# Rebuilding residual rows on ScalarE from kept norm statistics, and issuing their loads from SyncE

## The chip, the core and the metric

The kernel runs on one core of one Trainium2 chip. The metric is the device time of one execution in microseconds (us). Three timed runs of the kernel before gave 821.04, 821.12 and 822.54 us, so the median is 821.12 us. Each engine of the core has its own queue, worked in order: TensorE (PE in the profile, its weight loads PEld), VectorE (DVE), ScalarE (ACT), GpSimd (POOL) and SyncE (SP), which here only issues DMAs. An engine other than PE can issue DMAs too; the profile shows such issues as ACTq or SPq.

## The reference

One decoder layer with three sub-layers, on 512 rows of width 1024, each of the form `h <- LayerNorm(ALPHA * h + f(h))`, behind a first norm:

```python
def layer_norm(x, g, b):
    xf = x.astype(jnp.float32)
    mu = jnp.mean(xf, axis=-1, keepdims=True)
    var = jnp.mean(jnp.square(xf - mu), axis=-1, keepdims=True)
    return ((xf - mu) * lax.rsqrt(var + LN_EPS) * g + b).astype(x.dtype)

    h = layer_norm(x, ln_in_g, ln_in_b)
    f = hybrid_mixer(h, ...)      # gated linear attention, indexed sparse attention, stick-breaking
    h = layer_norm(ALPHA * h + f, ln_mix_g, ln_mix_b)
    f = mem_attn(h, mem, w_mem_q, w_mem_kv, w_mem_o)          # 4 heads, 256 memory tokens
    h = layer_norm(ALPHA * h + f, ln_mem_g, ln_mem_b)
    f = sq_relu_mlp(h, w_up, b_up, w_down, b_down)            # hidden width 4096
    h = layer_norm(ALPHA * h + f, ln_ffn_g, ln_ffn_b)
```

What the change touches is the first `h`. It is used twice: transposed, as the input of all mixer projections, and much later in rows, times ALPHA, as the residual of the first sub-layer.

## The kernel before, in words

The 512 tokens are four tiles of 128 rows (NT = 4), the 1024 features eight tiles (NK = 8). An fp32 operand is split into a high part (`h_...`, fp32r) and a low remainder (`l_...`), and each product is three matmuls: high by high, high by low, low by high. Making the low part of a weight is a subtraction of a 128x1024 tile on DVE or POOL; the high part is a cast on ACT, POOL or DVE.

The program does not emit its instructions as it is written. `Program.record` and `either` (L172 on) collect every operation with its dependencies, a cost and a place in the written order; `issue` (L240 to L357) then plans greedily with those costs and emits each engine's queue in the planned order, all from L356. Some operations may run on two or three engines (`either`), and the planner picks the one that would end first. So a changed operation can move others, on every engine.

The stages in time order are: the first norm with its transposes (`x`, `ps_lt`, `h0T`) and the first projections (`ps_ik_iw`, `ps_iq`), to about 25 us; the mixer's attention groups to about 310 us, with the projections of the memory tokens woven into the end of them (`ps_vm`, `ps_km`, weights `kvv`, `kvk`); output projection and second norm (`ps_wo`); cross-attention over the memory (`ps_q`, `ps_ms`, `ps_mpt`, `ps_wmo`); third norm; the MLP (`ps_up`, `ps_dn`) to 812 us; the last norm.

The places that the change touches:

- `ln_hat` (L521): row statistics of a 128x1024 tile (two BN_STATS of 512 columns, one aggregation, an added epsilon on DVE, a power on POOL), then `center`, one DVE instruction over 128x1024 that subtracts the mean and multiplies by the scale `rs`. At the start it runs on `x_pg[t]` (L563), in place; `ln_transposed` (L529) transposes the result on PE, applies gain and shift (`h`, on ACT or DVE) and splits it into `h0T`.
- The residual (L1137 to L1144): since the rows of `x` were given up, each tile of `x` is loaded again into a page `res`, `ln_hat(p, "again")` repeats statistics and centering, and `gain_shift` (L1130) multiplies by a row of gains (`gbc_in`) and adds a row of shifts (`bbc_in`), each 128x1024.
- `gb_rows` (L548) loads such rows of gains and shifts for each of the four norms by a broadcast DMA issued by ScalarE; POOL scales them by ALPHA. `bd` (L1206) is one more such row.

Pages of 128x1024 come from one pool of 31; raw weight tiles (`r_...`) from a pool of four. A DMA into such a buffer waits at the head of its issuing engine's queue until the earlier user of the buffer is done.

Of the kernel before, what the change touches and what calls it, by code (L numbers as in the profile page):

```python
# [9 lines left out]
F32 = mybir.dt.float32  # L10
F32R = mybir.dt.float32r
U32 = mybir.dt.uint32
AF = mybir.ActivationFunctionType
OP = mybir.AluOpType
# [3 lines left out]
T, D = 512, 1024  # L18
# [346 lines left out]
def trunk_kernel(ctx: ExitStack, tc: tile.TileContext, x, mem, ln_in_g, ln_in_b, w_in, gate_w2,  # L365
# [3 lines left out]
    x, mem, out = x[0], mem[0], out[0]  # L369
# [5 lines left out]
    def pool(name, tag, bufs, space=None):  # L375
        kw = {"space": space} if space else {}
        got = ctx.enter_context(tc.tile_pool(name=name, bufs=bufs or 1, **kw))
        return VPool(got, tag, bufs, space is PSUM)

    cst = pool("cst", None, 0)  # L380
# [8 lines left out]
    nc = Program(real)  # L389
    slack = [0.0]  # L390

    def page(shape, dtype, name):
        return pages.tile([128] + shape, dtype, name)

    def temp(name, n=512, dtype=F32):
        return half.tile([128, n], dtype, name)
# [7 lines left out]
    def pool_tt(o, a, b, op):  # L404
        nc.gpsimd.tensor_tensor(o, a, b, op=op)
# [89 lines left out]
    x_pg = []  # L495
    for t in range(NT):
        p = page([D], F32, f"x{t}")
# [10 lines left out]
    def mean_scale(st, name):  # L508

        mv = tiny(2, "mv_" + name)  # L510
        nc.vector.bn_aggr(mv, st)
        ve = tiny(1, "ve_" + name)
        nc.vector.tensor_scalar(ve, mv[:, 1:2], EPS, None, op0=OP.add)
        rs = tiny(1, "rs_" + name)
        nc.gpsimd.tensor_tensor(rs, ve, mhalf[:, 0:1], op=OP.pow)
        return mv, rs

    def center(y, mv, rs):
        nc.vector.tensor_scalar(y, y, mv[:, 0:1], rs, op0=OP.subtract, op1=OP.mult)

    def ln_hat(y, name):  # L521

        st = small.tile([128, 2, 6], F32, "st_" + name)
        for c in range(2):
            nc.vector.bn_stats(st[:, c, :], y[:, 512 * c:512 * c + 512])
        mv, rs = mean_scale(st, name)
        center(y, mv, rs)

    def ln_transposed(hat, g, b, hT, t0, n):  # L529

        w = 128 * n
        for k0 in range(0, NK, 512 // w):
            kk = 512 // w
            ps = bank("ps_lt", (kk, w))
            for k in range(kk):
                for t in range(n):
                    nc.tensor.transpose(ps[:, k, 128 * t:128 * t + 128],
                                        hat[t0 + t][:, 128 * (k0 + k):128 * (k0 + k) + 128], ident)
            for k in range(kk):
                kt = k0 + k  # L540
                cols = slice(128 * t0, 128 * t0 + w)
                h32 = temp("h32")[:, :w]
                gs, bs = g[:, kt:kt + 1], b[:, kt:kt + 1]
                nc.either(("scalar", "activation", (h32, ps[:, k, :], AF.Identity), dict(bias=bs, scale=gs)),
                          ("vector", "tensor_scalar", (h32, ps[:, k, :], gs, bs), dict(op0=OP.mult, op1=OP.add)))
                split(hT[kt][:, 0, cols], hT[kt][:, 1, cols], h32)

    def gb_rows(g, b, scale, name):  # L548
        res = []
        for nm, v in (("g", g), ("b", b)):  # L550
            p = page([D], F32, f"{nm}bc_{name}")
            nc.scalar.dma_start(p, v.to_broadcast([128, D]))
            if scale != 1.0:
                nc.gpsimd.tensor_scalar(p, p, scale, 0.0, op0=OP.mult, op1=OP.add)
            res.append(p)
        return res

    def new_hT(name):
        return [page([2, T], F32R, f"{name}{k}") for k in range(NK)]


    hT = new_hT("h0T")
    for t in range(NT):  # L563
        ln_hat(x_pg[t], "in")
        if t % 2:
            ln_transposed(x_pg, *gb_cols["in"], hT, t - 1, 2)

# [126 lines left out]
    for j in range(1, NT):  # L694
# [3 lines left out]
        for h in range(IDX_H):  # L698
# [7 lines left out]
            else:  # L706
                nc.vector.scalar_tensor_tensor(acc[:, :n], r[:, :n], iw[:, j, h:h + 1], acc[:, :n],
                                               op0=OP.mult, op1=OP.add)
# [103 lines left out]
    for b in range(NT):  # L812
# [8 lines left out]
        v = gv[b // 2][:, b % 2, :]  # L821
# [308 lines left out]
    def gain_shift(hat, gb, t, later=0.0):  # L1130
        nc.clock += later
        any_tt(hat[t], hat[t], gb[0], OP.mult)
        any_tt(hat[t], hat[t], gb[1], OP.add)
        nc.clock -= later


    gb = gb_rows(ln_in_g[None, :], ln_in_b[None, :], ALPHA, "in")  # L1137
    res = []
    for t in range(NT):
        p = page([D], F32, f"res{t}")  # L1140
        nc.scalar.dma_start(p, x[128 * t:128 * t + 128, :])
        ln_hat(p, "again")
        res.append(p)
        gain_shift(res, gb, t)  # L1144
    h1T = new_hT("h1T")
# [5 lines left out]

    gemm_tok(mix, w_out, 0, NK, "wo", after_mix)
    gb = gb_rows(ln_mix_g, ln_mix_b, ALPHA, "mix")
    for t in range(NT):
        gain_shift(res, gb, t, GAIN_LATER)
# [3 lines left out]
    for h in range(MEM_H):  # L1159
# [10 lines left out]
        for t in range(NT):  # L1170
# [8 lines left out]
            p = temp("mp")  # L1179
# [22 lines left out]

    gemm_tok(oT, w_mem_o, 0, NK, "wmo", after_mem)
    gb = gb_rows(ln_mem_g, ln_mem_b, ALPHA, "mem")
    bd = page([D], F32, "bd")
    nc.scalar.dma_start(bd, b_down.to_broadcast([128, D]))  # L1206
    pool_tt(gb[1], gb[1], bd, OP.add)
    for t in range(NT):
        gain_shift(res, gb, t, GAIN_LATER)
# [207 lines left out]
```

## Time and profile before

| | value |
|---|---|
| median of three timed runs | 821.12 us (821.04 to 822.54) |
| the profiled execution | 822.55 us |
| its span, first to last instruction | 820.8 us |
| outside the span | 1.75 us |
| mean granted TensorE clock | 0.990 of full |
| PE busy | 790.4 us, 96% |
| DVE busy | 636.3 us, 78% |
| ACT busy | 328.0 us, 40% |
| POOL busy | 144.5 us, 18% |

The profiled execution is one run, 1.43 us over the median of the timed ones. All durations below are from it. Busy times add up what each engine worked on; a share of 96% for PE leaves 30.4 us of the span in which it ran no matmul.

### The profile page before, as it was taken

The numbers are of one execution on the slowest core, as the hardware profiler recorded it, in microseconds if no ns is written. First come the engines' busy times: TensorE is split into PE (matmuls) and PEld (weight loads), VectorE is DVE, ScalarE is ACT, GpSimd is POOL, SyncE is SP. The second block draws the span as 40 slices with busy tenths as digits, with TensorE's granted clock in tenths as the row PEclk, the third lists the DMA queues.
The fourth block names the chain that finished last, engine by engine and source line by source line (L and its number), as shares of the span: only waits on it lengthen the run. The fifth ranks groups of instructions, "written<-read, shape, count | busy, mean of one in ns | idle before, by whom it ended". The sixth has DMA issues, their size and how long they took to land.

```text
span 820.8 us, 11293 instructions
## 1 busy us (share of the span) xinstructions
PE 790.4 (96%) x4177; PEld 662.5 (81%) x4177; DVE 636.3 (78%) x1118; ACT 328.0 (40%) x631; POOL 144.5 (18%) x169
## 2 busy tenths in 40 slices
PE   7999999999999999999999989999999999899995
PEld 5998768777877888899788888888888888678884
DVE  7737999997649984776953778997777776798778
ACT  5506634577535540244340233223323332585430
POOL 5320141354622210120530120000000000110001
PEclk8999999999999999999999999999999999999998
DMA  8520331603244535041322025466546555467632
GB/s 232 145 54 15 100 94 27 180 9 102 70 139 162 159 139 155 27 127 54 129 77 78 26 78 164 133 216 201 184 148 211 202 167 170 147 214 243 195 126 103
DMA packets 99927, 106.70 MB, mean 130 GB/s; under 512 B 10448, under 2 KB 79136, under 8 KB 99872
## 3 DMA queue, kind: packets, MB, share of 16 engines
q1 hardware_dynamic: 97344, 99.00, 38.5%
q10 hardware_dynamic: 2528, 6.98, 2.5%
q8 instruction: 33, 0.54, 0.3%
q14 instruction: 22, 0.18, 0.1%
HBM read 94.69 MB, written 10.49 MB: 128 GB/s over the span
## 4 chain that ended last, share of the span: by engine, by line
PE 69%; DVE 16%; issue 3%; ACT 1%; POOL 1%; DVEq 0%; ACTq 0%; POOLq 0%
PE ps_up L356 21%; PE ps_dn L356 18%; PE ps_wo L356 5%; PE ps_wmo L356 4%; PE ps_q L356 4%; DVE acc L356 2%; DVE m L356 2%; PE ps_km L356 2%; DVE res L356 2%; PE ps_z L356 2%; PE ps_vm L356 2%; PE ps_dq L356 1%; DVE s L356 1%; PE ps_mo L356 1%; PE ps_ms L356 1%
## 5 line engine op out<-in xcount | busy, mean ns | idle before, releaser
L356 PE MATMUL ps_up<-h2T,h_up 128*128 128x512 f32 (+1 forms) x576 | 163.1, 368 | 0.4 <-POOL h2T L356 0.4
L356 PEld LDWEIGHTS ps_up<-h2T,h_up 128*128 128x128 f32 x576 | 105.4, 191 | 18.2 <-POOL h2T L356 0.6
L356 PE MATMUL ps_up<-h2T,l_up 128*128 128x512 f32 (+1 forms) x288 | 105.9, 368 | 0.0
L356 ACT ACTIVATE ur<-ps_up,gb_all 128x512 f32<-128x512 f32 x32 | 22.1, 690 | 103.6 <-PE ps_up L356 103.4
L356 PEld LDWEIGHTS ps_up<-h2T,l_up 128*128 128x128 f32 x288 | 55.0, 191 | 8.6
L356 PE MATMUL ps_dn<-h_dn,a 128*128 128x512 f32 x192 | 59.2, 389 | 0.0
L356 DVE TENSOR_TENSOR l_dn<-r_dn,h_dn 128x1024 fp32r<-128x1024 f32 (+1 forms) x44 | 45.2, 1027 | 4.9 <-ACT h_dn L356 3.5
L356 PE MATMUL ps_dn<-h_dn,ends 128*128 128x512 f32 x128 | 47.0, 390 | 0.7 <-DVE ends L356 0.7
L356 POOL TENSOR_TENSOR a<-keep,a 128x1024 fp32r<-128x1024 f32 x1 | 4.9, 4924 | 229.9 <-DVE l_dn L356 229.9
L356 PE MATMUL ps_q<-h1T,h_wmq 128*128 128x256 f32 (+1 forms) x192 | 44.7, 323 | 0.3 <-POOL h1T L356 0.3
L356 PEld LDWEIGHTS ps_dn<-h_dn,a 128*128 128x128 f32 x192 | 36.0, 188 | 7.4
L356 ACT ACTIVATE h<-ps_lt,gb_all 128x256 f32<-128x256 f32 x18 | 9.1, 566 | 80.3 <-PE ps_lt L356 80.3
L356 PE MATMUL ps_wmo<-h_wmo,oT 128*128 128x512 f32 x128 | 40.8, 393 | 0.0
L356 PE MATMUL ps_wo<-h_wo,mix 128*128 128x512 f32 x128 | 40.3, 392 | 0.0
L356 DVE TENSOR_TENSOR l_up<-r_up,h_up 128x1024 fp32r<-128x1024 f32 x31 | 37.8, 1223 | 1.9 <-ACT h_up L356 0.5
L356 PE MATMUL ps_dn<-l_dn,a 128*128 128x512 f32 x96 | 37.3, 389 | 0.0
L356 PEld LDWEIGHTS ps_q<-h1T,h_wmq 128*128 128x128 f32 x192 | 32.0, 190 | 2.8 <-POOL h1T L356 0.6
L356 DVE TENSOR_SCALAR h_up<-r_up 128x1024 fp32r<-128x1024 f32 x19 | 13.1, 692 | 22.7 <-PE ps_up L356 16.4
L356 PE MATMUL ps_q<-h1T,l_wmq 128*128 128x256 f32 (+1 forms) x96 | 30.7, 320 | 0.0
L356 PEld LDWEIGHTS ps_dn<-h_dn,ends 128*128 128x128 f32 x128 | 24.0, 188 | 6.1 <-DVE ends L356 1.2
L356 PEld LDWEIGHTS ps_wo<-h_wo,mix 128*128 128x128 f32 x128 | 24.0, 188 | 4.9
L356 PEld LDWEIGHTS ps_wmo<-h_wmo,oT 128*128 128x128 f32 x128 | 24.0, 188 | 4.8
(407 smaller groups left out, 2085.2 us busy)
## 6 DMA issues: line engine op xcount, KB each, us to landing
r_dn<-in_w_down_dram SPq DMA_DIRECT2D x48, 512.0 KB, 4.3
r_up<-in_w_up_dram SPq DMA_DIRECT2D x32, 512.0 KB, 4.2
r_t<-t SPq DMA_DIRECT2D x16, 512.0 KB, 4.1
r_kvv<-in_w_mem_kv_dram SPq DMA_DIRECT2D x8, 512.0 KB, 4.3
r_kvk<-in_w_mem_kv_dram SPq DMA_DIRECT2D x8, 512.0 KB, 3.6
r_wo<-in_w_out_dram SPq DMA_DIRECT2D x8, 512.0 KB, 4.6
r_wmq<-in_w_mem_q_dram SPq DMA_DIRECT2D x8, 512.0 KB, 5.2
r_wmo<-in_w_mem_o_dram SPq DMA_DIRECT2D x8, 512.0 KB, 3.2
```

Of the source, the lines that this page charges most:

```text
L356: f(*[real(a) for a in args], **{k: real(a) for k, a in kwargs.items()})
```

## The change

Four things are edited. The first norm now keeps, for each row tile, two columns `kept` = (scale, -mean * scale), made by two DVE instructions of one column right after the centering. The residual rows are no longer normalised again from their own statistics: after the load, one ScalarE instruction computes `scale * x + (-mean * scale)` in place. The loads of the residual rows and of the rows of gains and shifts, and of `bd`, are issued by SyncE, 13 DMAs in all. Tiles get a name of their own per row tile.

```diff
@@ ln_hat
         mv, rs = mean_scale(st, name)
         center(y, mv, rs)
+        kept = cst.tile([128, 2], F32, "kept_" + name)
+        nc.vector.tensor_scalar(kept[:, 1:2], mv[:, 0:1], rs, -1.0, op0=OP.mult, op1=OP.mult)
+        nc.vector.tensor_copy(kept[:, 0:1], rs)
+        return kept
@@ gb_rows
-            nc.scalar.dma_start(p, v.to_broadcast([128, D]))
+            nc.sync.dma_start(p, v.to_broadcast([128, D]))
@@ first norm
+    norms = []
     for t in range(NT):
-        ln_hat(x_pg[t], "in")
+        norms.append(ln_hat(x_pg[t], f"in{t}"))
@@ residual
         p = page([D], F32, f"res{t}")
-        nc.scalar.dma_start(p, x[128 * t:128 * t + 128, :])
-        ln_hat(p, "again")
+        nc.sync.dma_start(p, x[128 * t:128 * t + 128, :])
+        nc.scalar.activation(p, p, AF.Identity, bias=norms[t][:, 1:2], scale=norms[t][:, 0:1])
         res.append(p)
         gain_shift(res, gb, t)
@@ before the third norm
-    nc.scalar.dma_start(bd, b_down.to_broadcast([128, D]))
+    nc.sync.dma_start(bd, b_down.to_broadcast([128, D]))
```

The planner makes a new order out of this. On DVE, at the start of the program, from the centering of row tile 0 (`x_86`) to the first low parts of the transposed input (`h0T`), it was:

```order
L356 TENSOR_SCALAR x_86<-x_86,mv_in,rs_in 128x1024
L356 TENSOR_TENSOR l_ik_iw<-r_ik_iw,h_ik_iw 128x8x72
L356 TENSOR_SCALAR x_91<-x_91,mv_in,rs_in 128x1024
L356 BN_STATS st_in<-x_103 128x6
L356 TENSOR_TENSOR l_iq<-r_iq,h_iq 128x1024
L356 TENSOR_SCALAR h0T_203<-h_190 128x256
L356 TENSOR_SCALAR h0T_205<-h_197 128x256
L356 TENSOR_TENSOR h0T_203<-h_190,h0T_203 128x256
```

In the changed kernel the same stretch of DVE, between the same two points, is:

```order
L356 TENSOR_SCALAR x_86<-x_86,mv_in_147,rs_in_159 128x1024
L356 TENSOR_SCALAR kept_in_166<-mv_in_147,rs_in_159 128x1
L356 COPY kept_in_166<-rs_in_159 128x1
L356 TENSOR_TENSOR l_ik_iw<-r_ik_iw,h_ik_iw 128x8x72
L356 TENSOR_SCALAR x_91<-x_91,mv_in_157,rs_in_169 128x1024
L356 TENSOR_SCALAR kept_in_184<-mv_in_157,rs_in_169 128x1
L356 COPY kept_in_184<-rs_in_169 128x1
L356 BN_STATS st_in_187<-x_103 128x6
L356 TENSOR_SCALAR h_196<-ps_lt,gb_in 128x256
L356 TENSOR_SCALAR h_205<-ps_lt,gb_in 128x256
L356 TENSOR_SCALAR h_213<-ps_lt,gb_in 128x256
L356 TENSOR_SCALAR h_217<-ps_lt,gb_in 128x256
```

Two `kept` instructions stand ahead of row tile 1's centering and two behind it. The low part `l_iq` has left the stretch (POOL makes it, right behind its two powers), and four `h` tiles that stood on ACT or later on DVE now stand ahead of the first low part of `h0T`, which is the next instruction.

On SP, from the last weight of the mixer (`r_dv`) to the weights of the memory's keys (`r_kvk`), minus is before and plus is now; `r_kvv` are the weights of the memory's values:

```order
 L356 DMA r_dv<-in_w_in_dram 128x8x128
-L356 DMA r_kvv<-in_w_mem_kv_dram 128x2x512 x8
+L356 DMA r_kvv<-in_w_mem_kv_dram 128x2x512 x4
+L356 DMA gbc_in<-in_ln_in_g_dram 128x1024
+L356 DMA bbc_in<-in_ln_in_b_dram 128x1024
+L356 DMA res_2606<-in_x_dram 128x1024
+L356 DMA res_2608<-in_x_dram 128x1024
+L356 DMA res_2610<-in_x_dram 128x1024
+L356 DMA res_2612<-in_x_dram 128x1024
+L356 DMA r_kvv<-in_w_mem_kv_dram 128x2x512 x4
 L356 DMA r_kvk<-in_w_mem_kv_dram 128x8x128 x8
```

Six loads now stand in the middle of the eight `r_kvv` loads. The pages of `gbc_in` and `bbc_in` come free with the transposes of the memory tokens (`ps_mt`), those of `res` with the last readers of `h0T`, the `ps_dv` matmuls.

On DVE in the residual stage, from the first statistics of a residual tile to the first added shift, it was:

```order
L356 BN_STATS st_again<-res_2608 128x6
L356 TENSOR_TENSOR vm_2707<-ps_vm,vm_2687 128x512
L356 BN_STATS st_again<-res_2608 128x6
L356 TENSOR_TENSOR vm_2723<-ps_vm,vm_2711 128x512
L356 BN_AGGR mv_again<-st_again 128x2
L356 BN_STATS st_again<-res_2613 128x6
L356 TENSOR_TENSOR mix_2728<-ps_ol,mix_2728 128x256
L356 TENSOR_SCALAR ve_again<-mv_again 128x1
L356 BN_STATS st_again<-res_2613 128x6
L356 BN_STATS st_again<-res_2615 128x6
L356 TENSOR_SCALAR res_2608<-res_2608,mv_again,rs_again 128x1024
L356 TENSOR_TENSOR l_kvv<-r_kvv,h_kvv 128x1024
```

In the changed kernel DVE has there (`s` are attention scores, `vm` and `mix` results taken out of PSUM):

```order
L356 RECIPROCAL dst<-dst 128x1
L356 TENSOR_TENSOR res_2606<-res_2606,gbc_in 128x1024
L356 TENSOR_SCALAR s<-s,dst 128x128
L356 RECIPROCAL dst<-dst 128x1 x3
L356 TENSOR_SCALAR s<-s,dst 128x256
L356 TENSOR_SCALAR s<-s,dst 128x128
L356 TENSOR_SCALAR s<-s,dst 128x256
L356 TENSOR_TENSOR vm_2718<-ps_vm,vm_2700 128x512
L356 TENSOR_TENSOR vm_2730<-ps_vm,vm_2714 128x512
L356 TENSOR_TENSOR res_2608<-res_2608,gbc_in 128x1024
```

The statistics, the aggregation and the centering are gone from DVE, and the gain of a residual tile stands between attention instructions as soon as the tile has come. On ACT the four new 128x1024 instructions stand together, around one cast of a `kvv` weight, behind the first `mix` tile of that stretch.

## Rows read from the trace of the kernel before

**Rows 1.** The page, part 1: busy time, share and instructions of each engine.
```profile
PE 790.4 (96%) x4177; PEld 662.5 (81%) x4177; DVE 636.3 (78%) x1118; ACT 328.0 (40%) x631; POOL 144.5 (18%) x169
```

**Rows 2.** Windows: stretch, its length, busy us of each engine (instructions), clock, DMA share, GB/s.
```profile
10.00:25.00 15.00, 14.72 (x106) 14.09 (x105) 13.69 (x29) 9.70 (x19) 8.39 (x10) 0.82 0.73 198
13.40:15.30 1.90, 1.90 (x11) 1.90 (x10) 1.43 (x5) 1.74 (x6) 1.06 (x2) 0.51 0.88 242
25.00:60.00 35.00, 35.00 (x230) 33.72 (x230) 18.50 (x29) 9.95 (x19) 8.75 (x8) 1.00 0.36 98
227.00:247.00 20.00, 19.21 (x102) 14.84 (x100) 9.23 (x33) 7.94 (x26) 5.57 (x4) 1.00 0.48 148
235.00:245.00 10.00, 10.00 (x51) 7.32 (x50) 2.17 (x4) 2.52 (x7) 1.06 (x1) 1.00 0.57 155
235.00:305.00 70.00, 67.75 (x465) 56.79 (x464) 58.38 (x122) 33.17 (x77) 15.50 (x12) 1.00 0.48 152
245.00:255.00 10.00, 10.00 (x54) 7.11 (x53) 8.61 (x28) 6.30 (x17) 1.62 (x2) 1.00 0.68 259
390.00:410.00 20.00, 18.05 (x91) 14.91 (x90) 19.34 (x24) 6.21 (x14) 10.47 (x5) 1.00 0.36 132
```

**Rows 3.** Timeline of PE: start, us, instructions, [idle before, releaser].
```profile
10.93 2.82 PE L356 MATMUL ps_lt<-ident,x 128*128 128x128 f32 x12 [0.28 <-DVE x L356]
13.40 0.56 PE L356 MATMUL ps_ik_iw<-h0T,h_ik_iw 128*72 128x256 f32 x1
...
270.30 0.55 PE L356 MATMUL ps_pt<-ident,s 128*128 128x128 f32 x3 [1.04 <-DVE s L356]
...
288.21 0.52 PE L356 MATMUL ps_pt<-ident,s 128*128 128x128 f32 x3 [1.22 <-DVE dst L356]
...
403.65 0.75 PE L356 MATMUL ps_ms<-kms,qT 128*128 128x256 f32 x4 [1.21 <-DVE qT L356]
...
409.91 0.96 PE L356 MATMUL ps_mpt<-ident,mp 128*128 128x128 f32 x6 [0.75 <-DVE mp L356]
```

**Rows 4.** Tiles `res`, `mv_again`, `rs_again`: operation, count, ns min/median/max, first and last start.
```profile
L356 DVE BATCH_NORM_STATS2 st_again<-res x8: 641/679/687, 248.1 to 274.0; 128x6 f32<-128x512 f32 x8
L356 DVE BATCH_NORM_AGGREGATE mv_again<-st_again x4: 195/200/209, 251.1 to 275.3; 128x2 f32<-128x12 f32 x4
L356 DVE TENSOR_SCALAR ve_again<-mv_again x4: 131/142/150, 252.8 to 293.4; 128x1 f32<-128x1 f32 x4
L356 DVE TENSOR_SCALAR res<-res,mv_again,rs_again x4: 792/798/811, 254.1 to 295.0; 128x1024 f32<-128x1024 f32 x4
```

**Rows 5.** Timeline of ACT and DVE near the start: start, us, instruction.
```profile
9.57 1.05 ACT L356 CAST h_iq<-r_iq 128x1024 fp32r<-128x1024 f32 x1 [0.65 <-DMA r_iq<-in_w_in_dram]
10.06 0.81 DVE L356 TENSOR_SCALAR x<-x,mv_in,rs_in 128x1024 f32<-128x1024 f32 x1
...
13.20 0.75 DVE L356 TENSOR_TENSOR h0T<-h,h0T 128x256 fp32r<-128x256 f32 x2
...
14.66 1.00 DVE L356 TENSOR_SCALAR h<-ps_lt,gb_in 128x256 f32<-128x256 f32 x2 [0.47 <-ACT h L356]
...
18.43 1.22 DVE L356 TENSOR_TENSOR l_iq<-r_iq,h_iq 128x1024 fp32r<-128x1024 f32 x1
```

**Rows 6.** Timeline at 261 us: two low parts, one on POOL and one on DVE.
```profile
261.10 2.47 POOL L356 TENSOR_TENSOR l_kvk<-r_kvk,h_kvk 128x1024 fp32r<-128x1024 f32 x1
261.27 3.38 DVE L356 TENSOR_TENSOR l_kvk<-r_kvk,h_kvk 128x1024 fp32r<-128x1024 f32 x1
```

**Rows 7.** Timeline of SP and ACT: loads and casts of `kvv` weights, and ScalarE's load issues.
```profile
219.12 7.55 SPq L356 DMA_DIRECT2D r_kvv<-in_w_mem_kv_dram  x4
...
240.67 2.15 ACTq L356 DMA_DIRECT2D res<-in_x_dram  x4
...
252.33 1.98 ACT L356 CAST h_kvv<-r_kvv 128x1024 fp32r<-128x1024 f32 x2
```

**Rows 8.** Timeline of PE at 227 us: `ps_dv` matmuls that read `h0T`.
```profile
227.10 0.62 PE L356 MATMUL ps_dv<-h0T,h_dv 128*128 128x512 f32 x2
```

## The prediction

> **What bounds the kernel now.** I read the busy times first. PE is busy 790.4 of 820.8 us, so all its idle time is 30.4 us, and no edit that leaves PE's matmuls as they are can win more than that [rows 1]. The change leaves PE's matmuls as they are: only their order differs. So the question is not how many microseconds DVE loses, but in which stretches PE idles, and whether DVE is what it waits for there. The windows answer this. From 25 to 60 us PE is busy for the whole stretch, whatever DVE does beside it [rows 2]. The change touches three other stretches: the start (10 to 25 us, PE idle 0.28 us, but at a granted clock of 0.82), the residual stage (235 to 305 us, PE idle 70.00 - 67.75 = 2.25 us) and the first part of cross-attention (390 to 410 us, idle 1.95 us) [rows 2]. The rows of PE's own timeline say what these gaps are: two of 1.04 and 1.22 us before the transposes of scores, released by DVE, make up all of the 2.25; two of 1.21 and 0.75 us, released by DVE as well, make up the 1.95 [rows 3]. DVE is busy 58.38 of 70 us and 19.34 of 20 us there [rows 2]. These 4.2 us are the whole prize in those two stretches.
>
> **What goes, and what it is worth.** On DVE go 8 statistics of 0.679, 4 aggregations of 0.200, 4 additions of 0.142 and 4 centerings of 0.798 us: 5.43 + 0.80 + 0.57 + 3.19 = 10.0 us, all between 248 and 296 us [rows 4]. That is more than four times the 2.25 us that PE idles in the stage. Both gaps end with work in front of which DVE had other work to do, so a freer DVE would close them if nothing else moved; that is the one end, -2.25. But the planner moves the fill-in matmuls too: PE's new order has fewer key projections between a tile's scores and its transposes, so PE asks sooner for what DVE makes. The other end is one new gap like the smaller one, +1.04. I take -0.9: PE wins back 40% of the gaps, somewhat over the middle of the two ends.
>
> The four powers on POOL go as well; POOL is busy 15.50 of 70 us, nothing waits for it there [rows 2], 0.
>
> On ACT come four instructions over 128x1024. The nearest row is casts of that shape, two in 1.98 us [rows 7], so 4.0 us; ACT is busy 2.52 us of the 10 between 235 and 245, so they fit before its next work [rows 2]. They stand in an in-order queue ahead of score exponentials and copies of transposes. If a residual tile landed late, those would wait. The SP queue issues the residual loads when `ps_dv` is through with the `h0T` pages, at about 228 us [rows 8], some 13 us earlier than ACT did (240.67) [rows 7]. So 0.
>
> **What moves to SP.** Thirteen loads. The six in the middle of the `r_kvv` loads make the fifth to eighth `r_kvv` wait for the pages of the residual, until about 228 us; before, the last four went out from 219.12 on within 7.55 us [rows 7, 8]. The last two of them are cast at 252.33 [rows 7]. Ten transfers of 512 KB are then ahead, 5.24 MB. At the 259 GB/s that a busy stretch moved [rows 2] they need 20 us, and the last lands at 248, 4 us before its cast; at the 148 GB/s of 227 to 247 us [rows 2] they need 35 us and land at 263, 11 us late. DMA was busy only 48% in that stretch, so the lower number is demand and not a limit; I take the first and 0, and keep the second for a rival. The loads for the later norms stand ahead of one output weight or, for `gbc_mem`, `bbc_mem` and `bd`, of seven memory-output weights, 0 by the same reasoning.
>
> In cross-attention POOL's scaling of those rows can come earlier than it does now, and DVE, the releaser of both gaps [rows 3], works on tiles of the same shape. Ends: -1.95 (both gaps go) and +1.21 (one more of them). The order there changes only around one low part, so I take 0.
>
> **What is added at the start.** Here PE is the bound, from 13.40 us on without a gap [rows 2, 3], so what its first product loses stays lost. Term one: two `kept` instructions of one column lie ahead of tile 1's centering; a one-column instruction took 0.142 us [rows 4], so PE's twelve transposes at 10.93 us, which wait for that centering [rows 3], start 0.3 us later. Term two: four `h` tiles of 0.50 us each (two in 1.00) [rows 5] now stand ahead of the first low part of `h0T`, where `l_iq` of 1.22 and two short casts stood; the last `h` can end only after the transposes it reads, which end near 13.9. So the first low part starts at about 13.9 and not at 13.20 [rows 5]: 0.7 us, and PE's new order takes the high-by-low products of `ps_ik_iw` for one feature tile after the other, so it waits for each. Term three: the centering of the last tile has two more `kept` instructions and an `l_iq` of 1.22 us ahead of it [rows 5], of which PE can fill most with `ps_iq`; I take 0.5 of 1.5. Together 0.3 + 0.7 + 0.5 = +1.5. The low end is term one alone, +0.3.
>
> The high end comes from POOL. It makes `l_iq` now, right behind its powers, beside the centering of tile 1. Two low parts that met on POOL and DVE took 2.47 and 3.38 us, and the same instruction on DVE alone 1.22 [rows 5, 6]: the later one lost 2.2 us, nearly the whole of POOL's. If the centering of 0.81 us meets it so, PE starts 0.3 + 2.2 = 2.5 us late, and with the last term 3.0. The Trainium skill ("SBUF — State Buffer", section "Who interferes with whom") says that DVE and GpSimd share a pair of ports that one of them holds for a whole instruction, and that the one that issued first keeps it while the other blocks; the 3.38 us agree with that. By that rule the centering, if it issues first, is not delayed, and 1.5 stands; if POOL issues first, the high end does. POOL's `l_iq` needs the cast of `h_iq`, which ends at 10.62 us; the centering began at 10.06 and begins 0.3 later now [rows 5], still ahead of it, hence the first.
>
> While PE waits there, its granted clock stays where it was: 0.51 of full, the lower of the two levels (1.2 GHz), from 13.40 to 15.30 us, and 1.00 from 25 us on [rows 2]. If that rise shifts with the first product, it is in term one and two; I add nothing.
>
> **Sum.** +1.5 - 0.9 + 0 + 0 = +0.6 us. The profiled execution took 822.55 us, 820.8 of span and 1.75 around it; so 823.15 by its own measure. It lies 1.43 us above the median of the timed runs, and the median becomes 821.7 us. What a measurement of this kernel can tell from no change is about 0.2%, 1.6 us; the forecast is no measurable change.
>
> **Rivals.**
> Rival A, DVE's 10 us do pay: all four gaps close, and the start loses only its low end. -2.25 - 1.95 + 0.3 = -3.9, 817.2 us. For it: DVE releases all four gaps. Against it: the fill-in matmuls that hid work there move, and DVE has only other work to run into. 0.25, counting everything that gains more than 1.6 us.
> Rival B, slower: the start decides. POOL's `l_iq` or the four `h` tiles hold the first products for the full 3.0 us, and nothing comes back later: 824.1 us. It decides if PE's first `ps_ik_iw` starts later than 15 us. For it: the start is the one stretch where PE has nothing to fill a wait with. Against it: the order of issue above. 0.20.
> Rival C, slower by SP: the weights behind the residual loads are late. If the seventh and eighth `r_kvv` land after 252.3 us, PE waits for `ps_vm`; up to 11 us at the lower rate, 5 if half of it is filled: 826.7. 0.08, because DMA had room.
> My case 0.47, with its own range 820.0 to 823.3, from -1.1 to +2.2 around the median before.
>
> Faster by over 0.2%: 0.25 from A and 0.02 from the edge of my case, 0.27. Slower: B and C, 0.28. Same: 0.45. The range reaches down to 818.0, into A but not to its end, and up to 825.0, over B but not C; I leave out some 0.10 below and 0.08 above.
>
> **What would show it.** PE's first `ps_ik_iw` at 14.0 to 14.7 us where it was 13.40, and the first stretch without wait after it; if at or before 13.7, the start costs less than I say. PE idle between 235 and 305 us near 1.4 us: at 0.5 or less A is right about that stage, above 2.3 the planner took back what DVE gave. The four ACT instructions without a wait for their loads and ended before 246 us. The eighth `r_kvv` landed before its cast; a PE wait for `ps_vm` means C. PE idle in 390 to 410 us unchanged near 2. The forecast is wrong if the time leaves 818 to 825, or if it comes out right with a start that costs nothing and a residual stage that wins nothing.

## The result, and the profile after

The changed kernel takes 834.43 us (median of 4 runs, 834.10 to 835.63), the kernel before 821.63 us (4 runs, 821.04 to 822.54). The ratio is 1.0158, with a 95% interval of 1.0143 to 1.0173: 12.8 us slower. The forecast was 821.7 us, no measurable change, with a range of 818 to 825: the time lies 9.4 us above that range. The profiled execution took 834.14 us with a span of 832.4 us and a mean granted clock of 0.981.

The loss sits in three stretches. The start of the last matmul that writes a tile marks where each ends (the profile can list the instructions of one tile). The columns are: when the first projections are over; the length of the residual stage (last `ps_dv` to last `ps_km`); of cross-attention (last `ps_wo` to last `ps_ms`); of what follows (last `ps_ms` to last `ps_up`), all in us of one profiled execution.

| kernel | `ps_iq` over | `ps_dv` to `ps_km` | `ps_wo` to `ps_ms` | `ps_ms` to `ps_up` |
|---|---|---|---|---|
| before | 44.5 | 75.1 | 72.5 | 283.5 |
| after | 48.4 | 78.5 | 78.1 | 281.9 |

So +3.9, +3.4, +5.6 and -1.6: 11.3 of the 11.6 us by which the span grew. The -1.6 is no gain of the change. In both kernels PE waits about 2 us for `res` ahead of transposes of the third norm. In the profile of the kernel before, the clock is at half for about 3.4 us behind that wait; in the profile of the changed kernel it is not (PE's timeline and a window of 5 us, first before, then after):

```profile
474.64 0.63 PE L356 MATMUL ps_lt<-ident,res 128*128 128x128 f32 x4 [2.03 <-DVE res L356]
475.00:480.00 5.00, 5.00 (x32) 5.00 (x31) 4.17 (x7) 0.00 (x0) 1.49 (x1) 0.66 0.68 207
...
487.59 0.63 PE L356 MATMUL ps_lt<-ident,res 128*128 128x128 f32 x4 [2.05 <-DVE res L356]
488.00:493.00 5.00, 5.00 (x44) 5.00 (x43) 4.11 (x7) 0.00 (x0) 1.49 (x1) 1.00 0.69 217
```

It is so in all 17 profiles of this case: the wait is 2.0 to 2.1 us in each, the clock falls behind it in ten, and these ten are the ones in which `ps_ms` to `ps_up` takes 283.5 us or more. Without it the three losses add up to 12.9 us, and the medians differ by 12.8.

In each of the three stretches PE waits for DVE. In the residual stage and in cross-attention its clock is low for some microseconds behind the longest waits; at the start it is low already and rises later. The windows of the changed kernel, with the columns of [rows 2], of the start, the residual stage and cross-attention:

```profile
10.00:25.00 15.00, 13.78 (x88) 13.02 (x87) 14.06 (x34) 6.64 (x14) 8.76 (x6) 0.71 0.79 220
25.00:60.00 35.00, 33.44 (x228) 31.71 (x226) 18.09 (x30) 10.47 (x21) 16.14 (x15) 1.00 0.34 88
...
245.00:255.00 10.00, 6.74 (x34) 5.11 (x32) 7.92 (x18) 6.45 (x14) 6.31 (x4) 0.96 0.57 169
255.00:265.00 10.00, 9.54 (x39) 7.04 (x40) 6.70 (x10) 4.24 (x7) 0.15 (x1) 0.70 0.07 16
265.00:275.00 10.00, 8.45 (x42) 6.22 (x41) 9.25 (x16) 2.84 (x10) 4.33 (x3) 1.00 0.69 196
235.00:305.00 70.00, 64.73 (x420) 53.79 (x419) 51.32 (x108) 37.92 (x87) 20.91 (x13) 0.95 0.50 165
...
412.00:415.00 3.00, 0.00 (x0) 0.00 (x0) 3.00 (x3) 0.00 (x0) 0.33 (x1) 0.93 0.55 171
415.00:420.00 5.00, 4.80 (x13) 4.00 (x14) 4.20 (x14) 1.93 (x8) 0.00 (x0) 0.50 0.01 3
```

Where the kernel before was busy for all of 25 to 60 us, PE now idles 1.56 us, and from 235 to 305 us 5.27 us instead of 2.25 [rows 2] (3.04 from the last `ps_dv` on: two waits of 0.59 and 0.20 us lie ahead of 235). DVE did lose work there, 51.32 us against 58.38, and PE waits more. After the gaps the clock is 0.70 (255 to 265 us) and 0.50 (415 to 420): a matmul at half clock counts as busy, so the busy columns hide this part of the loss. The wait of 1.55 us at 271.38 is not followed by it: the clock is 1.00 from 265 to 275 us. The waits that make these gaps (engine and tile waited for, us, times, longest):

```profile
PE ps_ms L356 <- DVE qT L356: 4.9, 1, 4.9
PE ps_pt L356 <- DVE s L356: 3.2, 2, 1.7
...
PE ps_ik_iw L356 <- DVE h0T L356: 2.0, 2, 1.3
PE ps_pt L356 <- DVE dst L356: 2.0, 1, 2.0
```

**The start**, on the timeline of PE and then of DVE:

```profile
11.10 2.82 PE L356 MATMUL ps_lt<-ident,x 128*128 128x128 f32 x12 [0.45 <-DVE x L356]
13.59 0.54 PE L356 MATMUL ps_ik_iw<-h0T,h_ik_iw 128*72 128x256 f32 x1
...
15.12 0.49 PE L356 MATMUL ps_ik_iw<-h0T,h_ik_iw 128*72 128x256 f32 x1 [0.77 <-DVE h0T L356]
...
32.83 0.34 PE L356 MATMUL ps_ik_iw<-h0T,h_ik_iw 128*72 128x256 f32 x1 [1.28 <-DVE h0T L356]
```

```profile
12.71 2.02 DVE L356 TENSOR_SCALAR h<-ps_lt,gb_in 128x256 f32<-128x256 f32 x4 [0.88 <-ACT h L356]
14.65 2.43 DVE L356 TENSOR_TENSOR h0T<-h,h0T 128x256 fp32r<-128x256 f32 x7
```

The transposes begin 0.17 us later than in [rows 3], but the first low part of `h0T` only at 14.65 us, where it was 13.20 [rows 5]: the four `h` tiles stand ahead of it. PE's third product waits until 15.12.

**The residual stage**, on the timeline:

```profile
232.75 3.69 SPq L356 DMA_DIRECT2D r_kvv<-in_w_mem_kv_dram  x4
...
242.74 1.06 POOL L356 TENSOR_SCALAR h_kvv<-r_kvv 128x1024 fp32r<-128x1024 f32 x1 [12.55 <-DMA r_kvv<-in_w_mem_kv_dram]
...
247.14 3.21 DVE L356 TENSOR_TENSOR l_kvv<-r_kvv,h_kvv 128x1024 fp32r<-128x1024 f32 x2 [2.08 <-POOL h_kvv L356]
...
252.81 2.34 POOL L356 TENSOR_TENSOR res<-res,bbc_in 128x1024 f32<-128x1024 f32 x1 [3.53 <-DVE res L356]
252.98 2.79 DVE L356 TENSOR_SCALAR s<-s,dst 128x256 f32<-128x256 f32 x3
253.01 0.30 PE L356 MATMUL ps_pt<-ident,s 128*128 128x128 f32 x1 [2.04 <-DVE dst L356]
...
255.46 1.30 PE L356 MATMUL ps_pt<-ident,s 128*128 128x128 f32 x5 [1.68 <-DVE s L356]
...
271.38 0.30 PE L356 MATMUL ps_pt<-ident,s 128*128 128x128 f32 x1 [1.55 <-DVE s L356]
```

The load of the fifth `kvv` weight, the first of these four, is issued 13.6 us later than before [rows 7] (4 us of that is the start). It also takes longer: a `kvv` load landed 3.8 to 5.0 us behind its issue before, and up to 10.4 us behind it here, beside the six row loads (the tile's view of `r_kvv`). POOL waits 12.55 us for it, and the low parts of this weight and the next two reach DVE just ahead of the scores that PE wants transposed. Then three scalings of `s` take 2.79 us beside POOL's addition at 252.81; three of that shape took 0.79 us before, at 247.42.

**Cross-attention**, on the timeline from the first gains of the second memory head to the gap:

```profile
397.60 1.73 DVE L356 TENSOR_TENSOR res<-res,bbc_mix 128x1024 f32<-128x1024 f32 x1
...
398.23 2.02 POOL L356 TENSOR_SCALAR bbc_mem<-bbc_mem 128x1024 f32<-128x1024 f32 x1
...
399.25 2.06 DVE L356 TENSOR_TENSOR res<-res,gbc_mix 128x1024 f32<-128x1024 f32 x1
400.33 3.26 POOL L356 TENSOR_TENSOR bbc_mem<-bbc_mem,bd 128x1024 f32<-128x1024 f32 x1
...
401.84 2.83 DVE L356 TENSOR_TENSOR res<-res,bbc_mix 128x1024 f32<-128x1024 f32 x1
...
407.27 1.79 POOL L356 TENSOR_SCALAR h_wmo<-r_wmo 128x1024 fp32r<-128x1024 f32 x1 [3.68 <-PE ps_q L356]
408.07 5.34 DVE L356 TENSOR_TENSOR res<-res,gbc_mix 128x1024 f32<-128x1024 f32 x2
409.14 3.19 POOL L356 TENSOR_TENSOR l_wmo<-r_wmo,h_wmo 128x1024 fp32r<-128x1024 f32 x1
...
415.20 1.23 PE L356 MATMUL ps_ms<-kms,qT 128*128 128x256 f32 x4 [4.93 <-DVE qT L356]
```

The rows of the third norm (`gbc_mem`, `bbc_mem`, `bd`) are loaded earlier: ScalarE issued the first of them at 394.74 us before, SyncE issues it at 392.49 here, though the head runs 7.4 us later. POOL works on them 9.4 us earlier in the head, and each DVE gain or shift beside that work takes 1.7 to 2.8 us, where one alone takes 1.22. So DVE comes late to its last two gains, and these take 5.34 us beside POOL's cast and low part of an output weight (407.27 and 409.14). PE then waits 4.93 us for `qT`.

### The profile page after: what moved, and what is told of

The parts are those of the page before. It is cut to its first block, busy times and chain, and to the rows that moved or that the text cites. A ratio compares the mean times of both kernels' runs of the same rounds, so it can differ in the third digit from the quotient of the medians.

```text
span 832.4 us, 11293 instructions
## 1 busy us (share of the span) xinstructions
PE 795.3 (96%) x4177; PEld 666.7 (80%) x4177; DVE 630.3 (76%) x1105; ACT 326.9 (39%) x630; POOL 158.2 (19%) x171
## 4 chain that ended last, share of the span: by engine, by line
PE 72%; DVE 11%; issue 3%; DMA 1%; POOL 1%; ACT 0%; DVEq 0%; ACTq 0%; POOLq 0%
PE ps_up L356 20%; PE ps_dn L356 17%; PE ps_wo L356 5%; PE ps_q L356 4%; PE ps_wmo L356 4%; DVE res L356 3%; PE ps_km L356 3%; PE ps_z L356 2%; PE ps_gg L356 1%; PE ps_dq L356 1%; DVE acc L356 1%; PE ps_ms L356 1%; DMA r_kvv<-in_w_mem_kv_dram 1%; PE ps_o L356 1%; DVE m L356 1%
## 5 line engine op out<-in xcount | busy, mean ns | idle before, releaser
L356 PE MATMUL ps_q<-h1T,h_wmq 128*128 128x256 f32 (+1 forms) x192 | 46.4, 333 | 0.3 <-POOL h1T L356 0.3
```

Of the source, the lines that this page charges most:

```text
L356: f(*[real(a) for a in args], **{k: real(a) for k, a in kwargs.items()})
```

## The experiments

Each was run beside the kernel before on the same chip. In the cuts of code a name like `gains_and_shifts` stands for a list of operations. Theory T says that the three stretches are three causes: the plan of the start, made anew around the kept columns; weights queued behind the residual loads on SP; POOL's row work brought forward into DVE's.

### Halves of the change

Only the loads go to SP (`e1`); only the kept columns and the ScalarE instructions (`e2`).

```diff
 # e1, against the kernel before
-nc.scalar.dma_start(p, ...)        # gb_rows, residual rows, bd
+nc.sync.dma_start(p, ...)
 # e2, against the changed kernel
-nc.sync.dma_start(p, ...)          # the same 13 loads
+nc.scalar.dma_start(p, ...)
```

> Only the 13 loads go to SyncE; the residual rows are still normalised again on VectorE and nothing is kept. Theory T (three separate losses: the kept columns at the start +3.9 us, the weights queued behind residual loads on SyncE +3.4, the earlier rows of the third norm before the scores of the second memory head +5.6): start as before (first ps_ik_iw at 13.4, ps_iq over at 44.5), the residual stage about +3 and the second head about +5, in all 829 to 831 us. Rival R1 (the whole loss comes from the kept columns and what they shift): 821 to 823 us.

> Kept columns and residual rows on ScalarE, but all 13 loads issued by ScalarE as before. T: the start loses 3.9 us (ps_iq over at 48.4), the residual stage gains 0 to 2 us, the second head as before, in all 823 to 826 us. Rival R2 (the SyncE queue is the whole loss, and VectorE's freed time pays): 818 to 821 us.

`e1` took 823.79 us (ratio 1.0021, 1.0012 to 1.0030), `e2` 824.13 us (1.0025, 1.0011 to 1.0040). `e2` is where T put it; `e1` is not: I expected 829 to 831. Its start is that of the kernel before and cross-attention loses 4.3 us, as T says, but the residual stage takes 72.2 us, 2.9 less than before instead of 3 more. `e2` has 74.1 us there. So each half alone helps the residual stage, and together they cost it 3.4 us: the two ratios add up to less than a third of the loss. In `e1` PE is idle for 1.15 us of that stage instead of 3.04, and DVE has the first statistics of a residual tile at 239.39 us instead of 248.13; whether that is the whole reason for the 2.9 us was not tried. The plan of `e1` put only two of the four residual loads, with the two rows, ahead of the fifth and sixth weight, and POOL cast the fifth 5.6 us after the last `ps_dv`; in the changed kernel 9.1 us after.

### The kept columns, later and early

`e5` gives the eight one-column instructions a place 400 operations later in the written order, so that the planner makes the start as before. `e12` is `e5` with these eight emitted right behind their centerings after all, and nothing else moved.

```diff
 # e5, against the changed kernel
+        nc.clock += KEPT_LATER        # 400.0
         nc.vector.tensor_scalar(kept[:, 1:2], ...)
         nc.vector.tensor_copy(kept[:, 0:1], rs)
+        nc.clock -= KEPT_LATER
 # e12, against e5, on the planned order; behind(group, last) puts a group right behind one operation
+        for t in range(NT):
+            behind(kept_operations[t], centering[t])
```

> The changed kernel with the kept columns given a place 400 operations later in the written order, so that the plan of the start is that of the kernel before. T: ps_iq is over at 44.5 as before, the other two losses stay, 830 to 831 us. Rival R4 (the later gaps are a knock-on of the shift at the start): 821 to 824 us.

> On the kernel with the kept columns late (830.4 us). One difference: the eight one-column instructions of the kept columns stand right behind their centering again, as in the changed kernel, but every other instruction of the start keeps the order of the kernel before. Theory T (the plan that was made anew costs the 3.9 us, not the instructions): ps_iq is over at 44.5 to 45.2 us, 830 to 831.5 us. Rival R7 (the instructions ahead of the transposes cost it by delay and clock): ps_iq over at 47 us or later, 832.5 to 835 us.

`e5` took 830.40 us (1.0092, 1.0064 to 1.0121), and `ps_iq` is over at 44.5 us as before; the other two losses are there in full (79.2 and 78.1 us). They are no knock-on of the start. `e12` took 828.82 us (1.0080, 1.0065 to 1.0095), a little under what T said, with `ps_iq` over at 44.6. The instructions stand where the changed kernel has them and the loss is gone: it was the order made anew. One caution: in its profile the clock was full from 13.40 to 15.30 us, where before it was 0.51 [rows 2]; that is worth up to 0.95 us, so the instructions themselves cost between 0.1 and about 1 us.

### Two weights ahead of the six loads

```diff
 # e4b, against e5, on the planned order
+        behind(loads_of_rows, kvv_loads[5])     # the six loads go behind the sixth kvv weight
```

> On the kernel with the kept columns late (830.4 us). One difference: on SyncE the fifth and sixth load of kvv weights stand ahead of the six loads of residual, gain and shift rows. Theory T (weights late by the loads ahead of them): the first cast of the fifth kvv weight on GpSimd comes 3 us or more earlier, the PE waits for s and dst between 240 and 275 us fall from 5.4 us to under 2.5, the stage from ps_dv to the last ps_km takes 74 to 76 us instead of 79.2, 825 to 828 us. Rival R6 (VectorE's new order of scores, low parts and gains makes the gaps, whenever the weights come): stage 78 to 80 us, 829 to 831 us.

`e4b` took 825.67 us (1.0047, 1.0032 to 1.0062). The residual stage falls from 79.2 to 73.8 us, with no other instruction moved. POOL no longer waits for the load of the fifth weight, but for `ps_dv` as before (POOL's timeline, `e4b`, its next two casts of `kvv` weights):

```profile
230.17 1.06 POOL L376 TENSOR_SCALAR h_kvv<-r_kvv 128x1024 fp32r<-128x1024 f32 x1 [3.61 <-PE ps_dv L376]
...
237.68 1.05 POOL L376 TENSOR_SCALAR h_kvv<-r_kvv 128x1024 fp32r<-128x1024 f32 x1 [5.31 <-PE ps_vm L376]
```

In `e5` these casts began at 238.62, behind a wait of 12.35 us for the load, and at 241.93. The PE waits for `s` fell less than expected, to 3.0 us; the wait for `dst` went, and so did the stretch at low clock (from 0.66 to 1.00 between 250 and 260 us). The 5.4 us are the difference of two single profiles. `e9`, `e12`, `e14` and `e19` have the order of `e5` in this stage too, and it took 76.8 to 77.9 us in them, with less wait or a shorter stretch at low clock; so the price is 3.0 to 5.4 us. The medians give 4.7 us (`e5` to `e4b`) and 4.0 us (`e19` to `e20`, the same edit).

### The second memory head: order on DVE

`e3` puts the three gains and shifts that stand ahead of the second `qT` behind it. `e9` puts all four around it behind the head's last `mp`, `e11` does the same on `e1`.

```diff
 # e3, against the changed kernel; e9 against e5; e11 against e1
+        behind(gains_and_shifts, second_qT)      # e3
+        behind(gains_and_shifts, last_mp)        # e9, e11
```

> The changed kernel with one difference: on VectorE the three residual instructions (two gains, one shift) that stand ahead of the second qT of the second memory head are put right behind it. T: the wait of PE for qT falls from 4.9 us to 1 us or less, the clock does not fall there, 828 to 830 us. Rival R3 (VectorE and GpSimd together have too much work there, and the wait only moves to the next instruction, for example to the row maxima mst): 832 to 835 us.

> On the kernel with the kept columns late (830.4 us). One difference: the four VectorE instructions of gain and shift on the residual tiles 2 and 3 that stand around the second qT of the second memory head are put behind the last probability tile mp of that head, which no one needs soon. Theory T2 (VectorE is late there as a whole, since its gains and shifts lie beside GpSimd's work on rows and weights and are stretched by it, and putting one instruction forward only moves PE's wait): PE's waits of 5.0 us for qT and of 3.7 us for mp both go, the stage from ps_wo to the last ps_ms takes 72.5 us or less instead of 78.1, 823 to 826 us. Rival R5 (GpSimd's low part of the weights sets the end of the stage): the wait moves again, 829 to 831 us.

> The kernel with only the loads on SyncE (823.8 us), with the four gains and shifts of the second memory head put behind its last mp. T2: the residual stage keeps its gain of 2.9 us, the head loses nothing, 817.5 to 820 us, faster than the kernel before. R5: 822.5 to 824 us.

`e3` took 831.82 us (1.0111, 1.0092 to 1.0131), `e9` 828.39 us (1.0072, 1.0054 to 1.0090), `e11` 822.66 us (1.0011, 1.0001 to 1.0022). None got where T said. In `e3` the wait for `qT` went and PE waited 3.7 us for `mp`; in `e9` and `e11` it waited 3.7 us for `mpT`. The stage took 75.5, 75.3 and 75.6 us: about half of the loss back in `e3` and `e9` and 1.2 of 4.3 us in `e11`; the rest moved to the next tile that PE needs, as the rivals had it. I had also called the place behind `mp` harmless, which it isn't, since `mpT` stands there.

### The second memory head: POOL's work

`e14` puts POOL's three instructions on the rows of the third norm behind its last low part of the output weights. `e19` leaves them in place and lets ScalarE do the two scalings.

```diff
 # e14, against e5, on the planned order
+        behind(pool_rows_of_third_norm, last_l_wmo_on_pool)
 # e19, against e5: same place in the order, other engine
-        gpsimd.tensor_scalar(row, row, ALPHA, 0.0, op0=OP.mult, op1=OP.add)
+        scalar.activation(row, row, AF.Copy, scale=ALPHA)
```

> On the kernel with the kept columns late (830.4 us). One difference: GpSimd's three instructions on the rows of the third norm (gain row, shift row, shift plus bias row) stand behind its last low part of memory-output weights. The order on VectorE stays. Theory T3 (VectorE is late in the second memory head because these GpSimd instructions lie beside its gains and shifts and stretch them; the trace of the changed kernel has 1.73, 2.06 and 2.83 us where each took 1.22 before): these take 1.2 to 1.3 us each again, PE's wait for qT falls from 5.0 to 2.5 us or less, the stage from ps_wo to the last ps_ms takes 73 to 75 us instead of 78.1, 825.5 to 828 us. Rival R8 (the order on VectorE alone makes it late): the wait for qT stays above 4 us, 829 to 831 us.

> On the kernel with the kept columns late (830.4 us). One difference: the two scalings of the rows of the third norm (gain, shift) are done by ScalarE at the same place of the order, not by GpSimd; the addition of the bias row stays on GpSimd behind them. VectorE's order is the same to the instruction. Theory T3 (it is GpSimd's work lying beside VectorE's that makes VectorE late): the three gains and shifts around the oT tiles take 1.2 to 1.3 us each as with the rows late, the wait for qT is 2.5 us or less, the stage from ps_wo to the last ps_ms takes 71 to 74 us, and unlike there nothing is lost in the head behind it: 823 to 826 us. Rival R9 (the load rows or the low parts of weights set the head, whoever scales): the wait stays above 4 us, 829 to 831 us.

`e14` took 825.92 us (1.0056, 1.0035 to 1.0078). Cross-attention falls from 78.1 to 71.2 us, less than before the change; DVE's order is untouched. But `ps_ms` to `ps_up` grew to 288.4 us (283.5 before and in `e4b`, whose clock falls ahead of the MLP too), since the moved work now lies beside the next head's probabilities (timeline of `e14`):

```profile
427.11 2.36 POOL L377 TENSOR_TENSOR bbc_mem<-bbc_mem,bd 128x1024 f32<-128x1024 f32 x1
427.28 2.34 DVE L377 TENSOR_SCALAR mp<-mp,mst 128x256 f32<-128x256 f32 x1
...
429.73 0.35 DVE L377 TENSOR_SCALAR mp<-mp,mst 128x256 f32<-128x256 f32 x1
429.77 0.87 PE L377 MATMUL ps_mpt<-ident,mp 128*128 128x128 f32 x4 [1.56 <-DVE mst L377]
```

The same DVE instruction takes 2.34 us beside POOL's addition and 0.35 us behind it, and PE waits for it. `e19` took 824.88 us (1.0036, 1.0022 to 1.0049): the stage 72.1 us, and `ps_ms` to `ps_up` 283.6. DVE's rows in `e19`, in the order of the changed kernel:

```profile
394.49 1.22 DVE L377 TENSOR_TENSOR res<-res,bbc_mix 128x1024 f32<-128x1024 f32 x1
...
399.09 2.35 DVE L377 TENSOR_TENSOR res<-res,gbc_mix 128x1024 f32<-128x1024 f32 x2
401.36 1.22 DVE L377 TENSOR_TENSOR res<-res,bbc_mix 128x1024 f32<-128x1024 f32 x1
402.50 0.68 DVE L377 SCALAR_TENSOR_TENSOR qT<-ps_q,qT 128x512 fp32r<-128x512 f32 x1
```

Two gains in 2.35 us where it was 5.34, and `qT` without a wait of PE. With DVE's order unchanged, `e14` and `e19` take the loss of this stage away, so POOL's work beside DVE's makes it; a new order on DVE alone gave back half of it or less.

### All causes away, and the best version

`e15` is `e4b` with POOL's rows late and the four gains behind the head's last `oT`; `e18` is `e1` with these two moves; `e8` is `e2` with the kept columns late. `e20` is `e4b` with the two scalings on ScalarE, `e21` is `e1` with them.

```diff
 # e15, against e4b; e18, against e1, on the planned order
+        behind(gains_and_shifts, last_oT)
+        behind(pool_rows_of_third_norm, last_l_wmo_on_pool)
 # e8, against e2: the kept columns 400 operations later, as in e5
+        nc.clock += KEPT_LATER
 # e20, against e4b; e21, against e1: as in e19
-        gpsimd.tensor_scalar(row, row, ALPHA, 0.0, op0=OP.mult, op1=OP.add)
+        scalar.activation(row, row, AF.Copy, scale=ALPHA)
```

> The changed kernel with all its causes taken away: kept columns late, two kvv weights ahead of the six loads, GpSimd's rows of the third norm late, and the four gains and shifts of the second memory head behind that head's last oT. If the causes are these and add up (3.9, 5.4 and 5.6 us), the time is 817 to 821 us, and VectorE's freed 10 us show in the residual stage (ps_dv to the last ps_km 72 to 74 us). If a part of the loss has another cause: 822 to 826 us.

> The kernel with only the loads on SyncE, GpSimd's rows of the third norm late and the four gains and shifts behind the second head's last oT. T: the residual stage 72.2 us as with the loads alone, the head 71 to 72.5 us, 816 to 819.5 us, faster than the kernel before and without any of the edits on ScalarE. Rival: if the gain of the residual stage came from VectorE's order and is given back behind it, 821 to 823 us.

> Kept columns late and residual rows on ScalarE, but all 13 loads issued by ScalarE as before. T: no loss at the start, the residual stage 73.5 to 74.5 us (75.1 before, 74.1 with the kept columns early), the head as before, 819 to 821.5 us: VectorE's 10 us are worth 1 to 2 us at most. Rival (VectorE's 10 us pay in full once nothing else moves): 815 to 818 us.

> Kept columns late, two kvv weights ahead of the six loads, and the two row scalings on ScalarE: the changed kernel without its three causes, with no move of gains. T: start as before, the residual stage 73.8 us as with the weights first, the head 71 to 74 us: 818 to 822 us. If the causes do not add up: 823 to 826 us.

> The kernel with only the loads on SyncE (823.8 us), with the two row scalings on ScalarE. T3: the residual stage keeps 72.2 us, the head takes 71 to 74 us instead of 76.8: 817 to 821 us, faster than the kernel before by 1 to 5 us. R9: 823 to 825 us.

| kernel | us | ratio to before (95%) | `ps_dv` to `ps_km` | `ps_wo` to `ps_ms` | `ps_ms` to `ps_up` |
|---|---|---|---|---|---|
| e15 | 824.34 | 1.0028 (1.0016 to 1.0040) | 73.8 | 74.5 | 284.4 |
| e18 | 822.49 | 1.0005 (0.9995 to 1.0014) | 72.2 | 75.2 | 284.1 |
| e8 | 821.56 | 0.9998 (0.9989 to 1.0008) | 74.0 | 72.5 | 283.5 |
| e20 | 820.89 | 0.9988 (0.9980 to 0.9997) | 73.8 | 72.1 | 282.0 |
| e21 | 819.18 | 0.9964 (0.9951 to 0.9978) | 72.2 | 73.7 | 282.0 |

`e15` and `e18` missed: the gains behind `oT` delay the next head's `qT`, and PE waits 2.9 us for it in both. With the scalings on ScalarE instead of moved, `e20` gets all of the loss back and a little more: the three causes account for the whole of it. From `after` over `e5` and `e4b` to `e20` the ratio to before falls by 0.0066, 0.0045 and 0.0059, some 5.4, 3.7 and 4.9 us. The third step can hold a gain of its own, since POOL scaled these rows beside DVE in the kernel before too (two shifts took 4.05 us there, at 398.95); the kernel before with the scalings on ScalarE was not run. `e8` says what the idea of the change is worth with its side effects away: no measurable change. `e21`, which keeps the second statistics on DVE, is the best version, 0.36% faster than the kernel before. That gain sits in the residual stage (72.2 us against 75.1), which `e1` has as well; the scalings on ScalarE take back what `e1` lost in cross-attention. The 73.7 us of `e21` there hold 3.4 us at half clock behind a wait of 1.75 us for `mp`; in `e20` the same wait is not followed by it, and the stage takes 72.1.

## Why the prediction was wrong

In place of the terms +1.5, -0.9, 0 and 0 the runs show +3.9 at the start, about -1 for DVE's freed time, 3.0 to 5.4 for the loads on SP and +5.6 in cross-attention. Three terms failed, two of them put at nothing.

**The frame** held: PE's matmuls are the same and only its waits and its clock could move. But it capped only a gain, at 4.2 us. Nothing caps a loss, and I priced each new wait by the gaps that were there, about 1 us; the new ones are up to 4.93 us, and the low clock behind them comes on top.

**DVE's 10 us.** Taken at -0.9 us; in `e8` the residual stage is 1.1 us shorter and the whole not measurably. The size fits the stage; the whole time cannot be told from no change. The four ScalarE instructions take 1.23 us each and not 1.0 (the tile's view of the changed kernel), and no wait of PE in the residual stage of `e8` ends with ScalarE (2.4 us, all for DVE's `s` and `dst`).

**The start.** Taken at +1.5 us with a high end of 3.0; it is +3.9. The mechanism was right, two sizes were off. PE's new waits: 0.17 us at the transposes (I took 0.3), 0.77 for the first low part (0.7, though the low part itself came 1.45 later, at 14.65), and 0.28 and 1.28 for products of the later tiles, where I took 0.5. Together 2.5 us and not 1.5. And I said that the clock would add nothing beyond a shift. It was 0.50 from 13.40 us on until about 18.6 (0.85 in the window from 18.50 to 19.00), and before until 15.3: 3.3 us more at half speed, 2.6 of them with PE busy, so about 1.3 us. In `e2`, with the same order of the start, PE's waits are alike (0.85, 0.29 and 1.29 us), but the clock was full from about 14 us on, and the start lost 2.4 us. The high end that I took from POOL's `l_iq` beside the centering did not come: POOL began it at 10.55 us, 0.31 behind the centering, and the centering took 0.81 us as before.

**The loads on SP.** Taken at 0, and this is the step that failed first. I compared the landing of the eighth weight with the last cast in [rows 7] and found 4 us to spare. That much held: its cast, at 260.75 us, waited for nothing. But the fifth is needed sooner. In the kernel before, four casts on POOL and one on ACT had begun by 229.85 us, as the last `ps_dv` ran, and the last of the four did not wait for a load (POOL's timeline before):

```profile
229.85 1.05 POOL L356 TENSOR_SCALAR h_kvv<-r_kvv 128x1024 fp32r<-128x1024 f32 x1 [3.57 <-PE ps_dv L356]
```

Here POOL could begin the fifth only at 242.74, 9.1 us after the last `ps_dv`, where `e1` has 5.6. Rival C named the queue and then asked whether PE waits for `ps_vm`. It does not. The late weight piles its low parts on DVE in front of the scores, and PE waits for those. `e4b` shows the price: 5.4 us by its profile and that of `e5`, 3.0 to 5.4 by all that share an order.

**Cross-attention.** Taken at 0 with ends of -1.95 and +1.21; it is +5.6. I wrote that POOL's rows can come earlier and did not price what they would then lie beside. The price stood in [rows 6], 3.38 us against 1.22, and I used it for the start only. Three DVE gains and shifts stretched by 0.5 to 1.6 us, and two more by 3.0 us together, make the wait. The Trainium skill ("SBUF — State Buffer", section "Who interferes with whom") says that a DVE instruction with two SBUF inputs contends with a GpSimd instruction that reads SBUF, and that ScalarE never waits for either; the 2.06 and 2.83 us beside POOL, and 1.22 with the work on ScalarE in `e19`, agree.

**The chances.** I set out the rivals as alternatives, each with one cause. The places of B and C came true together, neither by its own sign, and the largest loss, in cross-attention, had no rival at all. Nor are the causes independent: each half of the change alone costs about 2 us, both 12.8, and the planner made another order for each.

**The signs.** The first `ps_ik_iw` came at 13.59 us, which I would have read as a start that costs less than I say; the waits lie behind it. PE was idle for 5.27 us from 235 to 305 us, above the 2.3 that I gave as the sign of a lost gain. The four ScalarE instructions had no wait for their loads and ended at 248.7 us instead of by 246, 4 us of which is the start.

What stays open: why the clock rose at about 13.0 us in one execution (`e12`), 14 in another (`e2`), 15.3 and 18.6 in two more at nearly the same start; and why the same wait of about 2 us ahead of the third norm's transposes is followed by 3.4 us at half clock, worth 1.5 us, in ten profiles and not in seven. Neither was tried.

## What to carry to other kernels

Before a load is moved to another engine's queue, list for each load behind it when its first consumer runs, not the last, and follow the late work to the engine that it will pile up on. A planner turns a 0.2 us edit into a new order, so price a change by what each engine has next to it in the new order, above all DVE beside POOL in stretches where PE waits for DVE. An engine with nothing to gain is no reason to free it: with all side effects away DVE's 10 us bought nothing that could be measured, while moving two scalings off POOL won 4.6 us (`e1` to `e21`).

## What the runs showed of the hardware

A DVE instruction of 0.35 us took 2.34 us beside a POOL addition (`e14`), and POOL's addition took 3.26 us in the changed kernel, where it began during a DVE gain, and 2.36 to 2.40 in `e14` and `e19`, where it began ahead of the DVE instruction beside it: the delay goes both ways. A PE gap of 4.93 us was followed by 6 us at 0.50 of the clock, about 3 us more, which no wait row shows. A gap of 2.0 to 2.1 us was followed by 3.4 us at 0.50 in ten of 17 profiles and by full clock in the other seven. A load of 512 KB landed 3.8 to 5.0 us behind its issue, and up to 10.4 us when ten such loads were issued within 8 us.
